# A decoder layer on one core: the FFN's weight chunks begin at eight different places in larger buffers

## The chip, the cores and the metric

The kernel runs on one core of one Trainium2 chip. The metric is the device time of one execution in microseconds (us), as the median of several runs; lower is better. One further execution was taken with the profiler, and all rows below come from it.

## What is computed

One layer with float32 inputs and outputs: 256 tokens, 1024 features. A mixer half (attention and a causal pooling, gated and projected) is added to x, and then the gated FFN that the change touches:

```
h2 = rmsnorm(x, norm_ffn_g)
up = causal_depthwise_conv(h2 @ w_up, conv_w, conv_b)      # w_up: 1024 x 5632
gate, val = jnp.split(up, 2, axis=-1)                      # 2816 each
return x + (jax.nn.silu(gate) * val) @ w_down              # w_down: 2816 x 1024
```

## The kernel before

**Three products for one.** The tensor engine works on `float32r` operands. Each float32 operand is split in two, a high part (rounded to `float32r`) and a low part (the rest), and each product is made of three matmuls: high by high, high by low and low by high (`mm3`, L88; for the down projection L635 to L637). All three add up in one PSUM tile.

**Chunks of weights.** All weights come as chunks of 128 partitions by 2048 float32 (8 KB in a partition), in the fixed sequence `order` (L97 to L107): first q, k and v, then p, g, pool, bp, ba and o of the mixer, then 22 chunks `up` and 11 chunks `dn` of the FFN, mixed. SyncE loads each into one of four `raw` buffers (`load`, L111). ScalarE writes the high part into one of four `whi` buffers (`next_high`, L140, calling `high`, L80), VectorE writes the low part into one of four `wlo` buffers (`next_low`, L151, calling `low`, L84), both in pieces of 1024 columns. `ahead` (L161) stands between the matmul groups and makes the next pieces, so that the split runs ahead of the tensor engine. `chunk` (L169) hands the two buffers of a chunk to the matmuls.

**The FFN loop** (L669). Step i makes two tiles of the up projection, gate and value (`up_tile`, L644): 8 slices of features by 3 matmuls each, so 48 matmuls in a step from one `up` chunk. In each the weights are the stationary operand (128 x 128, brought in by a weight load) and the activations `hhi` and `hlo` the moving one (256 columns). Then it makes the part of the down projection of step i - 3 (`down`, L627): 8 output tiles by 3 matmuls, so 24 matmuls from half of a `dn` chunk; here the weights are stationary too, and the activations `ah` and `al` move. Over the FFN that is 22 x 48 + 22 x 24 = 1584 matmuls. In the q, k and v stage (L278) the roles are the other way round: the activations `xhi` and `xlo` are stationary, and 512 columns of weights move.

**Places in memory.** As the program is built before the change, each `whi` and `wlo` buffer begins 64 bytes past a multiple of 128 bytes (448 past a multiple of 512), and each slice of weights in it lies a multiple of 512 bytes further on. The activations that meet them (`xhi`, `hhi`, `mh`, `poolh`, `ath`, `ah` and their low parts) begin 96 bytes past a multiple of 128 (480 past a multiple of 512). So weights and activations have always the same places against each other within 512 bytes.

Of the kernel before, what the change touches and what calls it, by code (L numbers as in the profile page):

```python
# [9 lines left out]
F32R = mybir.dt.float32r  # L10
# [4 lines left out]
P = 128  # L15
# [17 lines left out]
CH = 2048  # L33
# [19 lines left out]
FFN_AHEAD = 6  # L53
KREADY = 1
FIRST = 2
XCUTS = (1, 2, 4, 6, 8)


@with_exitstack
def hybrid_layer_kernel(ctx: ExitStack, tc: tile.TileContext, xq_d, par_d, wkv_d, wpg_d,  # L60
# [5 lines left out]
    whi_p = ctx.enter_context(tc.tile_pool(name="whi", bufs=WBUFS))  # L66
    wlo_p = ctx.enter_context(tc.tile_pool(name="wlo", bufs=WBUFS))
# [11 lines left out]
    def high(hi, src, scale=1.0):  # L79
        nc.scalar.activation(hi, src, AF.Copy, scale=scale)  # L80
# [16 lines left out]
    order = [("q", None)] * 2 + [("k", wkv_d[c]) for c in range(2)]  # L97
# [10 lines left out]
    raws, his, los = {}, {}, {}  # L108
# [14 lines left out]
    def raw(c, sl):  # L123

        return xq[:, 4 * c + sl.start // 512, S:] if order[c][0] == "q" else raws[c][:, sl]
# [10 lines left out]
    def oldest():  # L136

        return next((c for c in range(len(order)) if c not in spent), len(order))

    def next_high():  # L140
        if at[0] < len(pieces):
            c, sl, first, _ = pieces[at[0]]
            if c - oldest() >= WBUFS:
                return
            at[0] += 1
            if first:
                his[c] = whi_p.tile([P, CH], F32R, tag="whi", name=f"hi_{order[c][0]}{c}")
                los[c] = wlo_p.tile([P, CH], F32R, tag="wlo", name=f"lo_{order[c][0]}{c}")
            high(his[c][:, sl], raw(c, sl))

    def next_low(eager=False):  # L151
# [9 lines left out]
    def ahead(upto=0):  # L161

        next_high()
        next_low()
        if at[1] - sum(p[0] < used[0] for p in pieces) < upto:
            next_high()
            next_low()
# [23 lines left out]
    cut = 0  # L191
    for k in XCUTS:
        end = KD + k * (S + AW)
# [25 lines left out]
    for k in range(KD):  # L219
        if k == 0:  # L220
            nc.vector.tensor_scalar(xhi[:, k, :], xT[:, k, :], gmix[:, k:k + 1], None, op0=ALU.mult)
        else:
            high(xhi[:, k, :], xT[:, k, :], gmix[:, k:k + 1])
        low(xlo[:, k, :], xhi[:, k, :], xT[:, k, :], gmix[:, k:k + 1])
        next_high()
        next_low(eager=True)
# [83 lines left out]
    def to_heads(qg, t, dst, name):  # L310
        pq = bank(f"ps_t{name}{t}")
        flat = qg.rearrange("p h d -> p (h d)")
        for j in range(KA):
            nc.tensor.transpose(pq[:, j * P:(j + 1) * P], flat[:, j * P:(j + 1) * P], ident)
        nc.scalar.activation(dst[:, :, t * P:(t + 1) * P], pq.rearrange("p (j c) -> p j c", c=P), AF.Copy)
# [110 lines left out]
    def scores(hp):  # L426
        ps = ps2.tile([P, 2, 512], F32, tag="ps2", name=f"ps_s{hp}")
        for j in range(2):
            rows = slice(j * DH, (j + 1) * DH)
            nc.tensor.matmul(ps[:, j, P:3 * P], qT[rows, hp, P:S], kT[rows, hp, :], start=True, stop=True)  # L430
            nc.tensor.matmul(ps[:, j, 0:P], qT[rows, hp, 0:P], kT[rows, hp, 0:P], start=True, stop=True)
        sm = tmp.tile([P, 2, 3 * P], F32, tag="big", bufs=4, name=f"sm{hp}")
        nc.vector.tensor_tensor(sm, ps[:, :, 0:3 * P],
                                mask.rearrange("p a b -> p (a b)")[:, None, :].to_broadcast([P, 2, 3 * P]), ALU.add)
        mx = tmp.tile([P, 2, 2], F32, tag="mx", name=f"mx{hp}")
        for t in (1, 0):
            nc.vector.tensor_reduce(mx[:, t, :], sm[:, :, TOK[t]], axis=AX.X, op=ALU.max)
        nc.vector.tensor_scalar(mx, mx, -(DH ** -0.5), None, op0=ALU.mult)
        sums = tmp.tile([P, 2, 2], F32, tag="sums", name=f"sums{hp}")
        for j in range(2):  # L440
            for t in (1, 0):
                nc.scalar.activation(sm[:, j, TOK[t]], sm[:, j, TOK[t]], AF.Exp, bias=mx[:, t, j:j + 1],
                                     scale=DH ** -0.5, accum_out=sums[:, t, j:j + 1])
        rs = tmp.tile([P, 2, 2], F32, tag="rs", name=f"rs{hp}")
        nc.vector.reciprocal(rs, sums)
        for t in (1, 0):
            n = TOK[t].stop - TOK[t].start
            nc.gpsimd.tensor_tensor(sm[:, :, TOK[t]], sm[:, :, TOK[t]],
                                    rs[:, t, :, None].to_broadcast([P, 2, n]), ALU.mult)
        later(4, weigh, hp, sm)  # L450
# [46 lines left out]
    for n in range(2 * KD):  # L497
        if n == KREADY:
            for t in range(NT):
                to_heads(kg[t], t, kT, "k")  # L500
        if n >= FIRST and (n - FIRST) % 4 == 0:
            scores((n - FIRST) // 4)
        if n == 10:
            pool_maps()
            ahead()
        b, c = n // 2, n % 2
# [267 lines left out]
```

## Time and profile before

| | us |
|---|---|
| median of 3 runs | 350.35 (348.51 to 350.55) |
| the profiled execution, its own time | 348.69 |
| its span, first to last instruction | 346.9 |
| its time outside the span | 1.8 |
| TensorE busy (PE) / VectorE (DVE) / ScalarE (ACT) | 340.7 / 261.0 / 195.7 |

In the profile PE is a matmul and PEld a weight load, which runs beside matmuls. The duration shown for a matmul (0.28 us) reaches from its issue to the modelled end of its pipeline, and overlaps those of its neighbours. So the rate of the tensor engine is read from the start of one matmul to the start of the next, and over a long stretch: time from the first start to the last, by the number of matmuls between them.

### The profile page before, as it was taken

The numbers are of one execution on the slowest core, as the hardware profiler recorded it, in microseconds if no ns is written. First come the engines' busy times: TensorE is split into PE (matmuls) and PEld (weight loads), VectorE is DVE, ScalarE is ACT, GpSimd is POOL, SyncE is SP. The second block draws the span as 40 slices with busy tenths as digits, with TensorE's granted clock in tenths as the row PEclk, the third lists the DMA queues.
The fourth block names the chain that finished last, engine by engine and source line by source line (L and its number), as shares of the span: only waits on it lengthen the run. The fifth ranks groups of instructions, "written<-read, shape, count | busy, mean of one in ns | idle before, by whom it ended". The sixth has DMA issues, their size and how long they took to land.

```text
span 346.9 us, 6715 instructions
## 1 busy us (share of the span) xinstructions
PE 340.7 (98%) x2736; PEld 329.2 (95%) x2736; DVE 261.0 (75%) x411; ACT 195.7 (56%) x311; POOL 101.5 (29%) x111
## 2 busy tenths in 40 slices
PE   8999999999999999999999999999999999999996
PEld 6887899999899999999999999999999999999995
DVE  4969889787587585899699877776777777777643
ACT  4956534634748945665367655555555555646420
POOL 1007991112202034586232212121212121212230
PEclk9999999999999999999999999999999999999999
DMA  7985642465272651566257555464636363652003
GB/s 275 419 327 213 222 159 110 150 220 213 69 259 92 242 201 45 175 237 211 109 168 271 188 224 201 164 222 145 242 123 243 131 235 132 232 162 83 0 2 121
DMA packets 10254, 62.76 MB, mean 181 GB/s; under 512 B 1136, under 2 KB 2288, under 8 KB 3312
## 3 DMA queue, kind: packets, MB, share of 16 engines
q1 hardware_dynamic: 10224, 62.34, 49.5%
q8 instruction: 21, 0.34, 0.4%
q14 instruction: 9, 0.07, 0.1%
HBM read 61.29 MB, written 1.05 MB: 180 GB/s over the span
## 4 chain that ended last, share of the span: by engine, by line
PE 80%; DVE 10%; DMA 4%; ACT 2%; issue 2%; SPq 1%; POOL 0%; ACTq 0%
PE ps_up L93 11%; PE ps_up L94 11%; PE ps_up L92 11%; PE ps_d L636 6%; PE ps_d L637 6%; PE ps_d L635 6%; PE ps_g L92 4%; PE ps_g L94 4%; PE ps_g L93 4%; DMA raw_k<-in_wkv 4%; PE ps_v L278 3%; DVE lo_up L84 2%; DVE hlo L86 2%; PE ps_bp L92 1%; PE ps_ba L94 1%
## 5 line engine op out<-in xcount | busy, mean ns | idle before, releaser
L92 PE MATMUL ps_up<-hhi,hi_up 128*128 128x256 f32 x352 | 98.5, 280 | 0.0
L93 PE MATMUL ps_up<-hlo,hi_up 128*128 128x256 f32 x352 | 98.4, 279 | 0.1
L94 PE MATMUL ps_up<-hhi,lo_up 128*128 128x256 f32 x352 | 98.3, 279 | 0.0
L93 PEld LDWEIGHTS ps_up<-hlo,hi_up 128*128 128x128 f32 x352 | 66.2, 188 | 0.4 <-DVE hlo L86 0.4
L92 PEld LDWEIGHTS ps_up<-hhi,hi_up 128*128 128x128 f32 x352 | 66.2, 188 | 0.0
L94 PEld LDWEIGHTS ps_up<-hhi,lo_up 128*128 128x128 f32 x352 | 66.2, 188 | 0.0
L84 DVE TENSOR_TENSOR lo_up<-raw_up,hi_up 128x1024 fp32r<-128x1024 f32 x44 | 55.9, 1273 | 6.1 <-ACT hi_up L80 6.1
L618 POOL TENSOR_TENSOR c_v<-c_g,c_v 128x256 f32<-128x256 f32 x22 | 16.2, 738 | 120.8 <-DVE c_v L601 120.8
L636 PE MATMUL ps_d<-al,hi_dn 128*128 128x256 f32 x176 | 49.1, 279 | 0.0
L635 PE MATMUL ps_d<-ah,hi_dn 128*128 128x256 f32 x176 | 49.1, 279 | 0.0
L637 PE MATMUL ps_d<-ah,lo_dn 128*128 128x256 f32 x176 | 49.1, 279 | 0.0
L80 ACT ACTIVATE hi_up<-raw_up 128x1024 fp32r<-128x1024 f32 x44 | 44.9, 1045 | 0.0
L92 PE MATMUL ps_g<-xhi,hi_g 128*128 128x256 f32 x128 | 36.5, 285 | 0.0
L93 PE MATMUL ps_g<-xlo,hi_g 128*128 128x256 f32 x128 | 35.7, 279 | 0.0
L94 PE MATMUL ps_g<-xhi,lo_g 128*128 128x256 f32 x128 | 35.7, 279 | 0.0
L80 ACT ACTIVATE ah<-c_v 128x256 fp32r<-128x256 f32 x22 | 9.2, 418 | 45.8 <-POOL c_v L618 45.8
L637 PEld LDWEIGHTS ps_d<-ah,lo_dn 128*128 128x128 f32 x176 | 33.1, 188 | 0.0
L635 PEld LDWEIGHTS ps_d<-ah,hi_dn 128*128 128x128 f32 x176 | 33.1, 188 | 0.0
L636 PEld LDWEIGHTS ps_d<-al,hi_dn 128*128 128x128 f32 x176 | 33.1, 188 | 0.0
L606 DVE TENSOR_TENSOR u_v<-ps_up,R 128x256 f32<-128x256 f32 x22 | 9.3, 421 | 26.1 <-PE ps_up L94 26.1
L84 DVE TENSOR_TENSOR lo_dn<-raw_dn,hi_dn 128x1024 fp32r<-128x1024 f32 x22 | 27.8, 1264 | 0.4 <-ACT hi_dn L80 0.4
L642 POOL TENSOR_TENSOR al<-c_v,ah 128x256 fp32r<-128x256 f32 x22 | 23.0, 1045 | 11.6 <-ACT ah L80 11.6
(182 smaller groups left out, 815.8 us busy)
## 6 DMA issues: line engine op xcount, KB each, us to landing
raw_up<-in_wup SPq DMA_DIRECT2D x22, 1024.0 KB, 4.8
raw_dn<-in_wdn SPq DMA_DIRECT2D x11, 1024.0 KB, 4.8
raw_g<-in_wpg SPq DMA_DIRECT2D x8, 1024.0 KB, 4.8
raw_o<-in_wout SPq DMA_DIRECT2D x4, 1024.0 KB, 4.8
xq<-in_xq SPq DMA_DIRECT2D x3, 768.0 KB, 7.4
raw_v<-in_wkv SPq DMA_DIRECT2D x2, 1024.0 KB, 14.1
raw_p<-in_wpg SPq DMA_DIRECT2D x2, 1024.0 KB, 6.3
raw_bp<-in_wbp SPq DMA_DIRECT2D x2, 1024.0 KB, 4.8
```

The lines of the kernel that those rows point to most:

```text
L80: nc.scalar.activation(hi, src, AF.Copy, scale=scale)
L84: nc.vector.tensor_tensor(lo, src, hi.bitcast(F32), ALU.subtract)
L92: nc.tensor.matmul(out, sh, mh, start=start, stop=False, **kw)
L93: nc.tensor.matmul(out, sh, ml, start=False, stop=False, **kw)
L94: nc.tensor.matmul(out, sl, mh, start=False, stop=stop, **kw)
L278: nc.tensor.matmul(pt[t], sx[:, k, t * P:(t + 1) * P], wx[:, sl], start=k == 0 and sx is xhi and wx is hi, stop=k == KD - 1 and wx is lo)
L606: nc.vector.tensor_tensor(u, ps[:, 0:S], R2, ALU.mult)
L618: nc.gpsimd.tensor_tensor(uc[1], g[1], uc[1], ALU.mult)
L635: nc.tensor.matmul(o, hi[:, sl], acch[i], start=first, stop=False, skip_group_check=True)
L636: nc.tensor.matmul(o, hi[:, sl], accl[i], start=False, stop=False, skip_group_check=True)
L637: nc.tensor.matmul(o, lo[:, sl], acch[i], start=False, stop=i == KF - 1, skip_group_check=True)
L642: nc.gpsimd.tensor_tensor(accl[i], act_i, acch[i].bitcast(F32), ALU.subtract)
```

## The change

The tiles of `whi` and `wlo` become 32 columns (128 bytes) wider for all chunks, and each chunk takes a window of 2048 columns in its tile. For `up` and `dn` the window begins at one of eight offsets in turn, the first chunk of its kind at 0 bytes, the second at 32, then 16, 48, 8, 96, 64, 80 and again from 0; `up` and `dn` count apart. For all other chunks it begins at 0. The high and the low part of a chunk have the same offset.

```diff
 FIRST = 2
+
+SHIFT = (0, 32, 16, 48, 8, 96, 64, 80)
 XCUTS = (1, 2, 4, 6, 8)
...
             if first:
-                his[c] = whi_p.tile([P, CH], F32R, tag="whi", name=f"hi_{order[c][0]}{c}")
-                los[c] = wlo_p.tile([P, CH], F32R, tag="wlo", name=f"lo_{order[c][0]}{c}")
+                name = order[c][0]
+                turn = sum(order[i][0] == name for i in range(c))
+                off = SHIFT[turn % len(SHIFT)] // 4 if name in ("up", "dn") else 0
+                his[c] = whi_p.tile([P, CH + 32], F32R, tag="whi", name=f"hi_{name}{c}")[:, off:off + CH]
+                los[c] = wlo_p.tile([P, CH + 32], F32R, tag="wlo", name=f"lo_{name}{c}")[:, off:off + CH]
             high(his[c][:, sl], raw(c, sl))
```

As the programs are built, every engine runs the same instructions in the same order with the same waits, before and after; only addresses differ. The buffers now lie 8320 bytes apart instead of 8192, so each still begins 64 bytes past a multiple of 128. All activations move up by 1024 bytes and keep their place within any 1024. The `raw` buffers stay where they were.

How the 33 chunks of the FFN fall on the offsets (48 matmuls each):

| offset, bytes | weights begin, past a multiple of 128 | `up` chunks | `dn` chunks |
|---|---|---|---|
| 0 | 64 | 3 | 2 |
| 32 | 96 | 3 | 2 |
| 16 | 80 | 3 | 2 |
| 48 | 112 | 3 | 1 |
| 8 | 72 | 3 | 1 |
| 96 | 32 | 3 | 1 |
| 64 | 0 | 2 | 1 |
| 80 | 16 | 2 | 1 |

## Rows read from the trace of the kernel before

**Rows 1.** The page: busy time of each engine, its share of the span and its instructions, the busy share of TensorE and the granted TensorE clock in 40 slices of the span.

```profile
span 346.9 us, 6715 instructions
PE 340.7 (98%) x2736; PEld 329.2 (95%) x2736; DVE 261.0 (75%) x411; ACT 195.7 (56%) x311; POOL 101.5 (29%) x111
...
PE   8999999999999999999999999999999999999996
...
PEclk9999999999999999999999999999999999999999
```

**Rows 2.** The windows of the FFN: its entry, the first steps, the steady steps, the last down projections and the end. Columns: window, its length, busy time and instructions of each engine, granted clock, DMA share, GB/s.

```profile
core 0: us, PE busy (x) PEld busy (x) DVE busy (x) ACT busy (x) POOL busy (x), PEclk, DMA share, GB/s
156.60:166.20 9.60, 9.03 (x75) 8.60 (x74) 8.35 (x12) 4.82 (x6) 6.13 (x6) 1.00 0.62 215
166.20:181.05 14.85, 14.85 (x128) 14.82 (x127) 12.71 (x24) 8.00 (x14) 3.83 (x5) 1.00 0.33 111
181.05:332.25 151.20, 151.20 (x1298) 151.20 (x1297) 112.54 (x164) 87.72 (x129) 33.92 (x38) 1.00 0.49 174
332.25:343.60 11.35, 11.35 (x98) 11.17 (x96) 5.15 (x12) 1.44 (x3) 1.47 (x2) 1.00 0.18 59
```

**Rows 3.** The timeline of the matmuls at the first and at the last start of the steady stretch, in order of time. Columns: start, duration, engine, line, operation, tile and operands, shapes.

```profile
180.95 0.28 PE L94 MATMUL ps_up<-hhi,lo_up 128*128 128x256 f32 x1
181.06 0.28 PE L635 MATMUL ps_d<-ah,hi_dn 128*128 128x256 f32 x1
181.19 0.28 PE L636 MATMUL ps_d<-al,hi_dn 128*128 128x256 f32 x1
...
332.15 0.28 PE L94 MATMUL ps_up<-hhi,lo_up 128*128 128x256 f32 x1
332.26 0.28 PE L635 MATMUL ps_d<-ah,hi_dn 128*128 128x256 f32 x1
```

**Rows 4.** The timeline of the matmuls of the first k chunk, where the weights move in 512 columns; each row is two matmuls, and there are 12 such rows from the first to the last.

```profile
17.24 0.63 PE L278 MATMUL ps_k<-hi_k,xhi 128*128 128x512 f32 x2
17.70 0.63 PE L278 MATMUL ps_k<-hi_k,xlo 128*128 128x512 f32 x2
...
22.37 0.63 PE L278 MATMUL ps_k<-lo_k,xhi 128*128 128x512 f32 x2
22.84 0.50 PE L238 MATMUL ps_n<-ones,vn 128*128 128x1 f32 x4
```

**Rows 5.** The timeline of the weight loads around the token sums of the FFN's norm (`ps_n`), whose matmuls move a single column, so that the weight loads follow one another with almost nothing between them.

```profile
162.46 0.19 PEld L94 LDWEIGHTS ps_up<-hhi,lo_up 128*128 128x128 f32 x1
162.57 0.53 PEld L238 LDWEIGHTS ps_n<-ones,ss 128*128 128x128 f32 x4
163.02 0.19 PEld L92 LDWEIGHTS ps_up<-hhi,hi_up 128*128 128x128 f32 x1
```

**Rows 6.** Groups of weight loads by line and form. Columns: busy time, mean ns of one, idle time before. In the first three the stationary operand is weights, in the others activations (`xhi`, `ss`).

```profile
L92 PEld LDWEIGHTS ps_up<-hhi,hi_up 128*128 128x128 f32 x352 | 66.2, 188 | 0.0
L94 PEld LDWEIGHTS ps_up<-hhi,lo_up 128*128 128x128 f32 x352 | 66.2, 188 | 0.0
L635 PEld LDWEIGHTS ps_d<-ah,hi_dn 128*128 128x128 f32 x176 | 33.1, 188 | 0.0
...
L278 PEld LDWEIGHTS ps_k<-lo_k,xhi 128*128 128x128 f32 x16 | 3.0, 188 | 0.7
...
L238 PEld LDWEIGHTS ps_n<-ones,ss 128*128 128x128 f32 x4 | 0.5, 190 | 0.0
```

**Rows 7.** Groups of VectorE by line and form in the steady stretch, 181.05 to 332.25 us: the low parts, and the taps of the convolution, which read and write `c` from 4 (L600) or 8 bytes (L601) past where its tile begins.

```profile
L84 DVE TENSOR_TENSOR lo_up<-raw_up,hi_up 128x1024 fp32r<-128x1024 f32 x36 | 44.8, 1248 | 6.1 <-ACT hi_up L80 6.1
L84 DVE TENSOR_TENSOR lo_dn<-raw_dn,hi_dn 128x1024 fp32r<-128x1024 f32 x20 | 24.9, 1243 | 0.4 <-ACT hi_dn L80 0.4
...
L601 DVE SCALAR_TENSOR_TENSOR c_v<-u_v,par,c_v 128x254 f32<-128x254 f32 x18 | 8.7, 482 | 0.6
L600 DVE SCALAR_TENSOR_TENSOR c_v<-u_v,par,c_v 128x255 f32<-128x255 f32 x18 | 8.6, 478 | 0.0
```

**Rows 8.** The same view of the first 20 us: the same operation where all operands begin where their tiles do.

```profile
L86 DVE SCALAR_TENSOR_TENSOR xlo<-xq,xhi 128x256 fp32r<-128x256 f32 x8 | 3.8, 481 | 1.1 <-ACT xhi L80 1.1
```

**Rows 9.** Groups of ScalarE in the steady stretch: the high parts.

```profile
L80 ACT ACTIVATE hi_up<-raw_up 128x1024 fp32r<-128x1024 f32 x35 | 35.7, 1044 | 0.0
L80 ACT ACTIVATE hi_dn<-raw_dn 128x1024 fp32r<-128x1024 f32 x20 | 20.0, 1045 | 0.0
```

**Rows 10.** The chain of work that ended last, in order of time, at the FFN's entry. Columns: start, share of the chain in us, what.

```profile
149.95 1.13 DVE lo_up L84
...
152.17 0.61 DVE lo_up L84
...
154.60 1.35 DVE lo_up L84
...
159.47 1.35 DVE lo_up L84
160.82 0.22 DVE hlo L86
161.04 0.46 issue
161.50 2.90 DVE lo_up L84 x2
...
166.52 0.12 PE ps_up L92
```

## The prediction

> **What bounds the kernel now.** First the page [rows 1]: the tensor engine is busy for 340.7 of 346.9 us, the matmul row shows 8 and 9 tenths in all slices but the last, and the granted clock is 9 in every slice, that is the level of 2.4 GHz all the way. VectorE has 75% and ScalarE 56%. So the question for a change of addresses is first of all what it does to the rate of the matmuls, and only then what it does to the engines that write the buffers.
>
> Then the windows of the FFN, where the change is [rows 2]. In the steady steps, from 181.05 to 332.25 us, the tensor engine is busy for 151.20 of 151.20 us: no wait for weights, for activations or for PSUM. Here alone the time is purely the number of matmuls by the spacing of their starts. The timeline gives that spacing [rows 3]: the first matmul of the stretch starts at 181.06, and the one that opens the last down projections at 332.26. Between them lie 18 steps of 48 + 24 matmuls, 1296 in all; 151.20 us / 1296 = 116.67 ns. A matmul moves 256 columns, which at 2.4 GHz are 106.67 ns. So each matmul of the FFN costs 10.0 ns more than its columns, and this is the one thing that a better placed operand could win. Over the FFN's 1584 matmuls it is 15.8 us.
>
> Whose cost are the 10 ns? If they came from the weight load (one in each matmul) meeting the moving stream, they would be a sum for each weight load. The k stage tells this apart [rows 4]: there a matmul moves 512 columns for one weight load. 12 rows of two lie between 17.24 and 22.84 us: 5.60 us / 24 = 233.3 ns, against 213.3 ns for 512 columns. That is 20.0 ns more, twice the 10.0 ns, with the same single weight load, and it is exactly twice 116.67. So the loss goes with the columns that move, 35 cycles for 32 columns, and not with the loads. In this stage the weights (64 bytes past a multiple of 128) move and the activations (96 past) stand; in the FFN it is the other way round. The rate of a column is the same. So the loss does not ask, either, at which of these two places the moving operand begins.
>
> How near is the weight load to being the bound itself? The timeline of the norm's sums shows it nearly bare [rows 5]: its matmuls move one column, and from the first of its four loads at 162.57 to the load after them at 163.02 there are 0.45 us, 112.5 ns for a load, what little the single columns take included. So a load of 128 columns takes at most 112.5 ns of its port, and the matmuls' 116.67 ns cover it with a margin of 4.2 ns. This is small, and it is the number to watch. The shown durations do not differ by place: 188 ns for weights at 64 past, 188 for `xhi` at 96 past, 190 for the sums' `ss` at 96 past [rows 6].
>
> **The change part by part.** It adds no instruction and moves none, adds no wait and no byte of transfer: the `raw` buffers, their loads and the number of buffers stay. Five things can have a price.
>
> *The moving stream of the FFN.* The activations keep their places within 1024 bytes, so a stream whose cost goes with its own columns costs the same 116.67 ns: 0 us. From below, nothing can be taken off here unless the loss is a matter of both operands, which is the faster rival.
>
> *The weight loads.* At the offsets 0, 32, 64 and 96 the slices begin at 64, 96, 0 and 32 past a multiple of 128, all multiples of 32. A place 96 past is in the trace: the `ss` loads that gave the 112.5 ns lie there. So these 17 chunks (11 `up`, 6 `dn`) stay under 116.67: 0 us. At 16, 48, 80 and 8 (16 chunks, 11 `up` and 5 `dn`, 768 matmuls) no row shows a load. From below 0, since a load that is hidden cannot win anything. From above, a slice is 512 bytes, and a start out of line touches one more piece of memory: 17 pieces of 32 bytes for 16 make 112.5 x 17/16 = 119.5 ns, 2.9 over the stream, 768 x 2.9 = 2.2 us; 9 pieces of 64 for 8 make 126.6, 9.9 over, 7.6 us. Pieces of 64 fit badly, as `ss` at 96 past is already across them at 112.5. I take 0, since the nearest rows (188 against 190 ns for different places, and the same rate of the moving stream at two places) know no price for a place; 2.2 us is kept for the range.
>
> The Trainium skill, "SBUF — State Buffer", section "Specifications (TRN2)", speaks against the change: it gives SBUF lines of 16 bytes, and each access that crosses to a new line pays. By that page the starts at 8 bytes past a line (4 chunks) would touch 33 lines for 32, which with the row's 112.5 ns is an estimate of 116.0 ns, still under the stream's 116.67 and so nothing; all other offsets are whole lines. No row of this kernel shows a load out of line.
>
> *The low parts on VectorE.* They read and write the shifted buffers: 56 pieces and 69.7 us of the steady stretch [rows 7], in which VectorE has 112.5 of 151.2 us [rows 2]. It would take 38.7 us more, 55% on every piece, to make VectorE the bound. The convolution's taps, which begin 4 or 8 bytes past their tile, give the price: 478 ns for 255 and 482 ns for 254 elements [rows 7], against 481 for 256 in place [rows 8]. A few ns on 1245: 0 us in the steady steps. In the entry the chain runs over `lo_up` [rows 10], where there is no slack, but some seven pieces at a few ns make under 0.1 us.
>
> *The high parts on ScalarE*: 1044 ns each [rows 9], with 87.7 of 151.2 us busy. Even 10% on 55 pieces is 6 us of 63 us idle: 0 us.
>
> *The wider pitch.* All the mixer's chunks still begin 64 past a multiple of 128, only no longer at the same place in 512. The 35 for 32 held with the moving operand at 64 past and at 96 past, so another multiple of 128 should cost as little: 0 us.
>
> **The sum** is 0 us: a span of 346.9 us as now. The profiled execution took 348.69 us, 1.66 under the median of 350.35, and the runs lie from 348.51 to 350.55; a repeat of the same program thus scatters by some 2 us. I set the forecast at the median, 350.35 us.
>
> **The rivals.** *Faster: the loss is a meeting of the two operands.* All rows of before have weights and activations 32 bytes apart within 512. If the 10 ns came of that, any other distance might end it, and 28 of the 33 chunks get another distance. The weight load then is the bound at 112.5 ns: 4.2 ns x 28 x 48 = 5.6 us, 344.7 us. Over 1% (3.5 us) needs 18 of the 28 chunks. Against it stands the k stage: twice the loss with one load [rows 4]. For it, that the k stage has the same distance, so that the distance was never tried. The Trainium skill, "SBUF — State Buffer", section "Who interferes with whom", speaks against this rival as well: it gives TensorE two independent read ports, one for the moving operand and one for weight loads. The trace agrees as far as the loss goes with columns at 20.0 to 10.0 ns. Chance 0.11.
>
> *Slower: the weight load becomes the bound at the odd places.* The place is every matmul of the 16 chunks at 16, 48, 80 and 8 bytes; the margin is 4.2 ns. At 126.6 ns for a load it is 7.6 us, 358.0 us. It decides from 116.67 + 3500/768 = 121.2 ns on, that is from a load that is 8% slower. If only the 8-byte chunks (192 matmuls) suffer, it takes 18 ns over the stream for the same 1%. For it: the margin is small and no row has such a start. Against it: no place that the trace has shows a price. Chance 0.13.
>
> *The change does not do what it says* is no case here: `chunk` hands out the shifted windows themselves, so the high part, the low part and all matmuls of a chunk use them.
>
> **How the numbers follow.** Under 1% (3.5 us) a measurement of this kernel, whose runs scatter by 2 us, can hardly tell from no change. Forecast, no change: 0.76, own range 348.5 (the lowest run) to 352.6 (350.35 + 2.2). Slower 0.13, faster 0.11. The range runs from 347.0, where about half of the moved chunks have reached the load's rate (350.35 - 2.8, and the scatter), to 354.0, just past where the slower rival decides; it leaves out the full prices on both sides, together under 0.2.
>
> **What would show it.** In the profile after, the steady stretch should again hold 1296 matmuls in 151.2 us, and each chunk by itself should show 116.67 ns from start to start, whatever its offset. That is the finest test: eight offsets in one trace. If the slower rival holds, only the chunks at 16, 48, 80 and 8 (or 8 alone) show spacings above 116.67, and the starts of the weight loads, not the matmuls, set them. If the faster one holds, the chunks off offset 0 show less than 116.67, and the chunks at 0 in the same loop do not. The low parts should stay at 1245 ns and the high parts at 1044. What would make the prediction wrong is a spacing that differs by chunk; a change of the time with 116.67 everywhere would have to come from the entry (156.6 to 166.2 us) or from the scatter of the runs.

## The result, and the profile after

| | before | after |
|---|---|---|
| median, us | 350.24 (348.44 to 350.59, 9 runs) | 351.8 (9 runs, 8 of them from 351.55 to 351.84) |
| ratio after / before | | 1.0056, 95% interval 1.0037 to 1.0075 |
| profiled execution, its own time | 348.69 | 351.81 |
| its span | 346.9 | 350.0 |

The change makes the kernel 0.6% slower. Disturbed executions are left out of the comparisons: of the changed kernel one (417.96 us at a granted clock of 0.756), and of four kernels below, whose clock was full, those in the slower of two levels, which are told where they stand.

Before itself has two levels, some at 348.4 to 348.8 us and some at 350.1 to 350.6; 6 of these 9 runs lie at the upper. After has one. Against the lower level, in which the profiled execution of before lies, the change costs 3.2 us.

The page of after, busy time and granted clock (answers to [rows 1]):

```profile
span 350.0 us, 6715 instructions
...
PE 343.9 (98%) x2736; PEld 332.1 (95%) x2736; DVE 261.0 (75%) x411; ACT 195.8 (56%) x311; POOL 102.3 (29%) x111
...
PEclk9999999999999999999999999999999999999999
```

The same 2736 matmuls, at the same clock, take 3.2 us more of the tensor engine's busy time; VectorE and ScalarE are as they were to 0.1 us. The windows of the FFN, cut at the same matmuls as in [rows 2]:

```profile
core 0: us, PE busy (x) PEld busy (x) DVE busy (x) ACT busy (x) POOL busy (x), PEclk, DMA share, GB/s
156.60:166.20 9.60, 9.18 (x76) 8.77 (x75) 8.75 (x12) 4.82 (x6) 6.45 (x7) 1.00 0.64 217
166.20:181.77 15.57, 15.54 (x128) 15.49 (x129) 13.03 (x24) 8.03 (x15) 4.10 (x5) 1.00 0.35 118
181.77:335.09 153.32, 153.32 (x1298) 153.32 (x1297) 112.18 (x164) 87.73 (x129) 34.39 (x37) 1.00 0.48 172
335.09:346.50 11.41, 11.41 (x98) 11.40 (x96) 5.15 (x12) 1.44 (x3) 1.46 (x2) 1.00 0.17 57
```

In the steady stretch the tensor engine is again busy all the time: no wait has come in. The timeline of its matmuls (answers to [rows 3]), columns as there: the first matmuls of three `out` chunks of the mixer, which the change moves only by the pitch; the first of the steady stretch; of three `up` chunks the first matmul and the first one behind the chunk; and the last start of the stretch.

```profile
134.57 0.28 PE L94 MATMUL ps_out<-mh,hi_o 128*128 128x256 f32 x1
...
140.27 0.28 PE L94 MATMUL ps_out<-mh,hi_o 128*128 128x256 f32 x1
...
145.88 0.28 PE L94 MATMUL ps_out<-mh,hi_o 128*128 128x256 f32 x1
...
181.78 0.28 PE L640 MATMUL ps_d<-ah,hi_dn 128*128 128x256 f32 x1
...
193.11 0.28 PE L94 MATMUL ps_up<-hhi,hi_up 128*128 128x256 f32 x1
...
198.55 0.28 PE L640 MATMUL ps_d<-ah,hi_dn 128*128 128x256 f32 x1
...
227.04 0.28 PE L94 MATMUL ps_up<-hhi,hi_up 128*128 128x256 f32 x1
...
232.80 0.28 PE L640 MATMUL ps_d<-ah,hi_dn 128*128 128x256 f32 x1
...
261.38 0.28 PE L94 MATMUL ps_up<-hhi,hi_up 128*128 128x256 f32 x1
...
267.04 0.28 PE L640 MATMUL ps_d<-ah,hi_dn 128*128 128x256 f32 x1
...
335.10 0.28 PE L640 MATMUL ps_d<-ah,hi_dn 128*128 128x256 f32 x1
```

From 181.78 to 335.10 are 153.32 us, by 1296 matmuls 118.3 ns, against 116.67 before. So 2.12 us are lost in the stretch, 0.72 ahead of it (181.78 against 181.06) and 0.26 behind it (350.0 - 335.10 = 14.90 against 346.9 - 332.26 = 14.64): 3.1 us, the whole difference of the spans.

And the spacing differs by chunk. The chunk at 193.11 (offset 96) takes 5.44 us / 48 = 113.3 ns, less than any spacing of before; the one at 227.04 (offset 32) 5.76 / 48 = 120.0; the one at 261.38 (offset 96 again) 5.66 / 48 = 117.9. The two unshifted `out` chunks take 5.70 / 48 = 118.8 and 5.61 / 48 = 116.9: their buffers begin 64 and 192 past a multiple of 256. All `up` chunks from the third step on, in ns, from starts to the single ns (the rows above are rounded to 10 ns):

| offset, bytes | first turn | second | third |
|---|---|---|---|
| 0 | | 117.9 (0) | 116.8 (0) |
| 32 | | 120.0 (32) | 118.5 (160) |
| 16 | 119.9 (144) | 119.9 (16) | 119.9 (16) |
| 48 | 118.3 (48) | 120.0 (176) | 120.0 (176) |
| 8 | 117.7 (8) | 117.8 (8) | 118.4 (8) |
| 96 | 113.3 (224) | 117.8 (224) | 113.7 (96) |
| 64 | 118.2 (64) | 118.4 (64) | |
| 80 | 118.1 (208) | 117.8 (80) | |

In brackets stands the place of the chunk within 256 bytes as the program is built, counted from that of before. The buffers lie 8320 bytes apart, so every second one is 128 bytes further within 256, and the eight offsets become the thirteen places of this table. Two offsets with two spacings are simply two places each (32 and 160, 48 and 176); the 113.3 and 117.8 at 224 are two spacings of one place.

The low parts in the stretch (VectorE groups by line and form, answers to [rows 7]), 1244 ns against 1248 and 1243, rule VectorE out:

```profile
L86 DVE TENSOR_TENSOR lo_up<-raw_up,hi_up 128x1024 fp32r<-128x1024 f32 x36 | 44.7, 1244 | 6.1 <-ACT hi_up L82 6.1
L86 DVE TENSOR_TENSOR lo_dn<-raw_dn,hi_dn 128x1024 fp32r<-128x1024 f32 x20 | 24.9, 1244 | 0.4 <-ACT hi_dn L82 0.4
```

### The profile page after: what moved, and what is told of

The parts are those of the page before. It is cut to its first block, busy times and chain, and to the rows that moved or that the text cites. A ratio compares the mean times of both kernels' runs of the same rounds, so it can differ in the third digit from the quotient of the medians.

```text
span 350.0 us, 6715 instructions
## 1 busy us (share of the span) xinstructions
PE 343.9 (98%) x2736; PEld 332.1 (95%) x2736; DVE 261.0 (75%) x411; ACT 195.8 (56%) x311; POOL 102.3 (29%) x111
## 4 chain that ended last, share of the span: by engine, by line
PE 80%; DVE 10%; DMA 3%; ACT 2%; issue 2%; SPq 1%; POOL 0%; ACTq 0%
PE ps_up L95 11%; PE ps_up L94 11%; PE ps_up L96 11%; PE ps_d L640 6%; PE ps_d L642 6%; PE ps_d L641 6%; PE ps_g L94 4%; PE ps_g L95 4%; PE ps_g L96 4%; DMA raw_k<-in_wkv 3%; PE ps_v L283 3%; DVE lo_up L86 2%; DVE hlo L88 2%; PE ps_bp L94 1%; PE ps_ba L96 1%
## 5 line engine op out<-in xcount | busy, mean ns | idle before, releaser
L647 POOL TENSOR_TENSOR al<-c_v,ah 128x256 fp32r<-128x256 f32 x22 | 23.8, 1080 | 11.6 <-ACT ah L82 11.6
```

What stands on the lines that cost most here:

```text
L647: nc.gpsimd.tensor_tensor(accl[i], act_i, acch[i].bitcast(F32), ALU.subtract)
```

## The experiments

The theory (P) is that the spacing is set by the place of the weights against the moving activations, and that one place can hold more than one spacing. The rivals: a price only for starts that are out of line with some piece of memory; a price for changing the place from chunk to chunk; contention from the engines that write the buffers (E); and chance, a spacing that asks for no place. "Offset" below is counted from where the weights begin in before; unless said, the activations keep their place within 256 bytes. A run of before stands beside each group: 348.77 (19 runs), then 348.73 (9), 348.69 (8) and 349.04 (11) us.

**The kernel before again**, no edit.

> The kernel before, unchanged, for a second trace of it. Theory P (place): a matmul's spacing follows from where its weights begin against its moving activations within some power of two of bytes, 256 as the trace after suggests; here all chunks have one place, so every chunk should show 116.67 ns again, as in the first trace. Theory S (state): the spacing wanders from execution to execution whatever the places; then this trace shows chunks at 117 to 120 ns as the changed kernel did.

348.82 us in one run, 116.67 ns in each chunk behind the FFN's entry. Of the 19 runs of before beside it, 7 lie at 350.26 to 350.48 us and 12 at 348.60 to 348.91.

**The pitch alone**, without an offset.

```diff
-his[c] = whi_p.tile([P, CH], F32R, ...)
+his[c] = whi_p.tile([P, CH + 32], F32R, ...)[:, 0:CH]        # lo the same
```

> Tiles 32 columns wider as in the change, all windows at 0: the buffers lie 8320 bytes apart, so two of the four begin 192 and two 64 bytes past a multiple of 256 (activations: 224). Theory P: chunks in the buffers at 192 stay at 116.67 ns, chunks in those at 64 take 117.4 to 118.8 ns, as the mixer's unshifted chunks do after the change; over some 1584 FFN and 800 mixer matmuls, half of them, that is 1 to 2 us more: 351 to 352.5 us. Rival Q (only the starts out of line by 8 or 16 bytes cost, by way of the weight load): no chunk changes, 350.2 us.

349.92 us (349.82 to 350.08, 10 runs), ratio 1.0019 (1.0 to 1.0037). That is over a microsecond less than expected: 6 of the 18 `up` chunks in the steady stretch, and not half of them, lie in a buffer at 64, and they take 117.3 or 118.7 ns. Two neighbouring `up` chunks, first matmul and the first one behind each:

```profile
235.05 0.28 PE L92 MATMUL ps_up<-hhi,hi_up 128*128 128x256 f32 x1
...
240.65 0.28 PE L635 MATMUL ps_d<-ah,hi_dn 128*128 128x256 f32 x1
...
243.50 0.28 PE L92 MATMUL ps_up<-hhi,hi_up 128*128 128x256 f32 x1
...
249.20 0.28 PE L635 MATMUL ps_d<-ah,hi_dn 128*128 128x256 f32 x1
```

5.60 / 48 = 116.7 ns in a buffer at 192 past a multiple of 256, 5.70 / 48 = 118.8 in one at 64. Both are 64 past a multiple of 128, so that is not the measure; and starts that are all multiples of 64 bytes differ, so no penalty on odd starts is needed.

**A pitch that keeps the place within 256 bytes**: as above with `CH + 64`.

> Tiles 64 columns wider, all windows at 0: the buffers lie 8448 bytes apart, a multiple of 256, and the activations move up by 2048 bytes. Theory P: all chunks keep their place within 256 bytes and stay at 116.67 ns; the time is that of the kernel before, 348.4 to 350.6 us. Rival R (larger buffers, a wider pitch or moved activations cost by themselves): at least as slow as the change, 351.8 us.

350.22 us (348.55 to 350.49, 10 runs), ratio 1.0009 (0.9986 to 1.0032): the two levels of before, with one run between them (349.48). Its profiled execution (350.26 us) lies in the upper one, the first and last matmul of the steady stretch:

```profile
181.07 0.28 PE L635 MATMUL ps_d<-ah,hi_dn 128*128 128x256 f32 x1
...
333.71 0.28 PE L635 MATMUL ps_d<-ah,hi_dn 128*128 128x256 f32 x1
```

152.64 us / 1296 = 117.8 ns, where before had 116.67 at the same place within 256 bytes. So the upper level of this kernel is a second spacing of one place: 1.1 ns more in the FFN's 1584 matmuls is 1.7 us, the distance of the levels. A trace of before's own layer in it comes with the groups of several sizes below.

**The place by itself**: behind the FFN, with no other engine at work, groups of 48 matmuls (their products unused) on one chunk, at 32 offsets, 8 bytes apart, in two orders.

```diff
+    for turn in (1, 13):
+        for g in range(32):
+            off = 2 * (g * turn % 32)
...
+            for k in range(48):
+                nc.tensor.matmul(pr[:, 0:S], hw[:, k % 8 * 128 + off:k % 8 * 128 + off + P], hhi[:, k % 8, :], start=True, stop=True)
```

> The kernel before with 64 groups of 48 matmuls added behind the FFN, at a time when no other engine works: the moving operand is hhi (224 past a multiple of 256), the stationary one a window of the last chunk's high part that begins 0, 8, ... 248 bytes further, once in ascending order and once in steps of 104 bytes. Their products are used by nothing. Theory P: the spacing differs from group to group between 113 and 120 ns with no other engine at work, and mostly agrees between the two orders. Rival Q: 116.67 ns at all multiples of 32 and more at the others. Rival E (other engines' traffic in the buffers makes the difference): 116.67 ns or less in all groups.

`off` counts elements of 4 bytes. The timeline of some groups in the first order (each row one group, the letter ahead of the `b` its offset: a is 0, b 8, e 32, f 40, m 96, n 104):

```profile
343.19 5.77 PE L709 MATMUL probe_ab<-hhi,hi_dn 128*128 128x256 f32 x48
348.79 5.81 PE L709 MATMUL probe_bb<-hhi,hi_dn 128*128 128x256 f32 x48
...
365.71 5.91 PE L709 MATMUL probe_eb<-hhi,hi_dn 128*128 128x256 f32 x48
371.46 5.71 PE L709 MATMUL probe_fb<-hhi,hi_dn 128*128 128x256 f32 x48
...
411.23 5.62 PE L709 MATMUL probe_mb<-hhi,hi_dn 128*128 128x256 f32 x48
416.69 5.85 PE L709 MATMUL probe_nb<-hhi,hi_dn 128*128 128x256 f32 x48
```

From one group's start to the next: 5.60 us at 0, 5.75 at 32, 5.46 at 96, which is 116.7, 119.8 and 113.8 ns with what lies between two groups; inside a group 116.67, 120.0 and 113.3. Over all places 113.3 (96, 120 and 200 in both orders) to 120 (32, 136, 144, 192, 248), once 121.6 (56, in the other order 118.6) and once 123.3 (8, in the other order 117.8). At 224 the two orders gave 117.8 and 113.3, as the change did. The whole range of the FFN's spacings is here with VectorE and ScalarE at 0.00 us of work and a DMA share of 0.00 (from 347.5 us to the end), so the rival E falls; and among the places with 120 are multiples of 64 and 32 (192, 32) as well as of 8 alone (136, 248).

**One offset for the whole FFN**, the best and the worst of the change's own, at the pitch that keeps the place.

```diff
+off = 24 if order[c][0] in ("up", "dn") else 0
+his[c] = whi_p.tile([P, CH + 64], F32R, ...)[:, off:off + CH]     # lo the same
```

24 elements are 96 bytes; the other kernel has 8 for 32 bytes.

> Tiles 64 columns wider (the buffers keep one place within 256 bytes) and all up and dn chunks at one offset, 96 bytes; the mixer's chunks at 0. The probe showed 113.33 ns at this offset in both orders. Theory P (the place of the weights against the moving activations, within 256 bytes, sets which repeating pattern of spacings the matmuls fall into): the FFN runs at 113.33 ns throughout, 3.3 ns less on 1584 matmuls, 5.3 us less: 343.5 us if the kernel before is in its 116.67 pattern at 348.6 us, 1.8 us more gain against its 117.83 pattern. Rival Q (weight loads at odd starts): no gain can come from a start, 348.5 us or more. Rival T (it is the changing from place to place that costs, not the place): 116.67 as before, 348.6 to 350.5 us.

343.81 us (343.71 to 343.95, 4 runs), ratio 0.9861 (0.9846 to 0.9875). The first and last matmul of the stretch:

```profile
180.74 0.28 PE L636 MATMUL ps_d<-ah,hi_dn 128*128 128x256 f32 x1
...
327.78 0.28 PE L636 MATMUL ps_d<-ah,hi_dn 128*128 128x256 f32 x1
```

147.04 us / 1296 = 113.5 ns. It is faster than both kernels.

> As the run with 96 bytes, but all up and dn chunks at 32 bytes, where the weights begin at the same place within 128 bytes as the activations. The probe showed 120.0 ns in both orders. Theory P: 120.0 ns throughout the FFN, 3.3 ns more on 1584 matmuls, 5.3 us more than the 116.67 pattern: 353.9 us. Rival T: 116.67 ns, 348.6 to 350.5 us. Rival Q: the start is a multiple of 32, so no change.

353.72 us (353.56 to 353.74, 4 runs), ratio 1.0144 (1.0128 to 1.0159), the same rows:

```profile
181.46 0.28 PE L636 MATMUL ps_d<-ah,hi_dn 128*128 128x256 f32 x1
...
336.98 0.28 PE L636 MATMUL ps_d<-ah,hi_dn 128*128 128x256 f32 x1
```

155.52 us / 1296 = 120.0 ns. A start at a multiple of 32 bytes that never changes costs more than the change with its eight offsets: neither a price for odd starts nor one for changing places says that. Two kernels that differ in 64 bytes of place are 9.9 us apart.

**The activations moved instead**, weights as in before, so that the difference is that of offset 96.

```diff
+gap = ctx.enter_context(tc.tile_pool(name="gap", bufs=1)).tile([P, 40], F32, name="gap")
```

The gap is 160 bytes and lies ahead of the activations.

> Weights and their buffers as in the kernel before; a gap of 160 bytes ahead of the activations moves all of these, so that weights begin 64 bytes past the activations within 256, the same difference as with weights moved by 96. If only the difference counts: 113.33 ns in the FFN and in the mixer (g, p, bp, ba, o), 3.3 ns less on some 2400 matmuls, 8 us less: 340.5 us. If the place of the weights by itself counts: 116.67 ns, 348.6 us. If that of each operand by itself counts, some other spacing.

343.05, 343.15 and 343.36 us, and 349.83 and 349.89; ratio from the first three 0.9844 (0.9825 to 0.9864). The profiled execution is one of the latter:

```profile
180.72 0.28 PE L636 MATMUL ps_d<-ah,hi_dn 128*128 128x256 f32 x1
...
333.36 0.28 PE L636 MATMUL ps_d<-ah,hi_dn 128*128 128x256 f32 x1
```

152.64 us / 1296 = 117.8 ns, at a clock of 0.998. The same execution had 113.3 ns in the mixer. The first of the 96 matmuls of `ba`, and the first one behind them:

```profile
122.80 0.28 PE L93 MATMUL ps_ba<-ath,hi_ba 128*128 128x256 f32 x1
...
133.68 0.28 PE L93 MATMUL ps_out<-mh,hi_o 128*128 128x256 f32 x1
```

10.88 us / 96 = 113.3 ns. So the gain comes by moving either operand: the difference counts, not the place of the weights. And this difference has two spacings, 113.3 and 117.8. In this execution the one gave way to the other at the FFN's entry, where waits and the sums of the norm break the stream. The better times are some 2.7 us over the 340.5 that were expected, which counted the mixer's matmuls at full gain: even with 113.3 ns in the mixer the FFN began only 1.0 us earlier than in before (155.69 against 156.66).

**Size and repetition**, groups as above: load widths of 128, 64 and 32 columns, 256, 512 and 128 moving columns, both operands moved together, and one place again and again behind 1 to 10 short matmuls.

```diff
+            w = k % 8 * 128 + off // 4
+            m = k % (1536 // n) * n + mo // 4
+            nc.tensor.matmul(pr[0:cols, 0:n], hw[:, w:w + cols], wide[:, m:m + n], start=True, stop=True)
```

> The kernel before with groups of matmuls added behind the FFN, whose products nothing uses. Offsets of the weights 0, 32 and 96 bytes; weight loads of 128, 64 and 32 columns for 256 that move; 512 that move; 128 that move; both operands moved together by 32, 64 and 128 bytes; and repeats of one place with another number of short matmuls ahead of each. Theory C (the reads of the weight load and of the moving operand collide, and the place decides how often): with loads of 64 and 32 columns the spacing falls towards 106.7 to 109 ns and no longer depends on the offset; with both operands moved together the spacing stays that of the difference; repeats at one place show a few fixed values (116.67 and 117.83 at offset 0). Theory M (the moving stream loses 3 cycles in 32 columns by itself, as the prediction had it): 116.67 ns for shorter loads too. At 512 columns the prediction's 233.3 ns should come back at offset 0; theory C has the same loss for one load whatever moves, so about 223 ns, unless a load spreads over the longer stream.

Some of the groups (a is offset 0, b 32; `full` is 128 columns loaded and 256 moved, `half` and `quarter` load 64 and 32, `long` and `short` move 512 and 128; `again_c` is offset 96):

```profile
363.11 5.76 PE L711 MATMUL probe_long_a<-hhi,hi_dn 128*128 128x512 f32 x24
368.70 5.47 PE L711 MATMUL probe_short_a<-hhi,hi_dn 128*128 128x128 f32 x48
374.01 5.96 PE L711 MATMUL probe_full_b<-hhi,hi_dn 128*128 128x256 f32 x48
379.80 5.61 PE L711 MATMUL probe_half_b<-hhi,hi_dn 128*64 128x256 f32 x48
385.25 5.61 PE L711 MATMUL probe_quarter_b<-hhi,hi_dn 128*32 128x256 f32 x48
390.69 5.63 PE L711 MATMUL probe_long_b<-hhi,hi_dn 128*128 128x512 f32 x24
396.16 5.47 PE L711 MATMUL probe_short_b<-hhi,hi_dn 128*128 128x128 f32 x48
...
522.75 3.04 PE L711 MATMUL probe_again_c<-hhi,hi_dn 128*128 128x256 f32 x24
525.91 2.95 PE L711 MATMUL probe_again_c<-hhi,hi_dn 128*128 128x256 f32 x24
```

At offset 32 the full group takes 5.79 us to the next start, `half` and `quarter` 5.45 and 5.44: inside the groups 120.0 against 113.3 and 113.3 ns. The moving columns are the same, so the weight load takes part in the loss. How is not so simple: at offset 0 the three widths gave 117.8, 119.0 and 117.3 ns, at 96 all three 113.3, so the spacing still goes with the offset and does not fall to 106.7 to 109 ns, as theory C had it. 512 columns take about 227 ns at offset 32 and 233 at 0 and 96. 128 columns take 5.31 us / 48 = 110.6 ns at offset 0, near the bare load of [rows 5]. With both operands moved together by 32, 64 and 128 bytes, difference 0 gave 116.67 or 117.8, difference 32 gave 120 and difference 96 gave 117.8 each time (unmoved 113.3, its other spacing): again the difference. Repeated ten times, offset 0 gave 116.67 eight times and 117.8 twice, offset 96 gave 113.3 eight times and 117.8 twice, offset 224 gave 117.8 ten times: the two rows of `again_c`, 3.04 and 2.95 us for the same 24 matmuls, are 0.09 / 23 = 4 ns apart for each spacing. So one place has few spacings, and a stream takes up one of them where it begins.

The layer ahead of these groups is that of before, to the address. Its FFN, the first and the last start of the steady stretch:

```profile
182.16 0.28 PE L635 MATMUL ps_d<-ah,hi_dn 128*128 128x256 f32 x1
...
334.80 0.28 PE L635 MATMUL ps_d<-ah,hi_dn 128*128 128x256 f32 x1
```

152.64 us / 1296 = 117.8 ns, behind a mixer at 116.67: the second spacing of before, in a trace of its own. The matmuls ahead of the FFN are the same in all executions of before, so they alone do not pick the spacing.

**The change's offsets at the pitch that keeps the place**: the change with `CH + 64` for `CH + 32`.

> The change with tiles 64 instead of 32 columns wider: the eight offsets as they were, but all buffers at one place within 256 bytes. Theory P: the mixer back at 116.67 ns; in the FFN each chunk at a spacing that the probe showed for its offset (113.3 at 96, 116.7 at 0, 117.3 to 118.3 at 16, 8, 48, 64 and 80, 120 at 32; by the number of chunks at each, 117.5 on average), 1.3 us over the 116.67 pattern: about 349.9 us, and two chunks of one offset may show two spacings. If the offsets alone make the whole loss of the change: 351.8 us.

350.98 us (350.78 to 351.27, 5 runs), ratio 1.0061 (1.0041 to 1.008): 1.1 us over what was expected: in the profiled execution (351.27 us) the chunks at 16 bytes ran at 119.6 to 119.9 ns where the groups had 117.3, and at 96 bytes one of three `up` chunks and the `dn` chunk at 117.7 to 117.9 for 113.3. Over the lower level of 348.6 us the pitch alone costs 1.3 us, the offsets alone 2.4, both 3.2: they don't add, because the pitch changes the places at which the offsets fall.

**One offset for all chunks**, the mixer's too: `off = 24`, `30` or `50` (96, 120 and 200 bytes, the three places with 113.3 in both orders).

> Tiles 64 columns wider and all chunks, the mixer's too, at 96 bytes. Theory P with two patterns at this place (113.33 and 117.79 ns): where the 113.33 pattern holds in the FFN and in most of the mixer, 341 to 343.5 us; in executions in which the FFN falls into the other one, about 349.9 us as in the run with moved activations. If weights moved forward and activations moved by the rest of 256 are the same thing, the times and patterns of that run come back.

343.45, 343.56 and 343.57 us, and 350.15; ratio from the first three 0.9846 (0.9817 to 0.9874). The profiled execution is the last, with 117.8 ns throughout the FFN: the two levels of the kernel with moved activations.

> As the run with all chunks at 96 bytes, but at 120, where the probe showed 113.33 ns in both orders. Theory P: 113.33 ns in FFN and mixer, 341 to 343 us. Rival Q (starts that are no multiple of 32 slow the weight load): slower than 348.6 us.

342.94, 343.05, 347.47 and 348.31 us, ratio without the last 0.9873 (0.9801 to 0.9945). Two of the four are some 5 us over the 341 to 343 that were expected. The profiled execution, 348.31 us, has 116.7 ns in the FFN and the mixer, where the groups had 113.3 at this place.

> As the run with all chunks at 96 bytes, but at 200, where the probe also showed 113.33 ns in both orders. Theory P: 113.33 ns in FFN and mixer, 341 to 343 us; if the place has a single pattern, all executions within 0.3 us of each other. Rival Q: slower than 348.6 us.

355.48 us (354.37 to 355.66, 4 runs), ratio 1.018 (1.0146 to 1.0215): a miss, by 12 us. The stretch:

```profile
183.11 0.28 PE L636 MATMUL ps_d<-ah,hi_dn 128*128 128x256 f32 x1
...
338.63 0.28 PE L636 MATMUL ps_d<-ah,hi_dn 128*128 128x256 f32 x1
```

155.52 us / 1296 = 120.0 ns, where the groups alone had 113.3 at the same place. A place does not have one spacing, and a short stream of one sequence does not tell which one the kernel gets.

**The entry**: the FFN's own sequence (weights by activations: high by high, high by low, low by high), 24 matmuls at 8 offsets, entered behind 1, 2, 3, 5 and 7 short matmuls, with 128, 64 and 32 columns loaded.

```diff
+            w, mv = ((hw, hhi), (hw, hlo), (lw, hhi))[k % 3]
+            at = k // 3 * 256 + off // 4
+            nc.tensor.matmul(pr[0:cols, 0:S], w[:, at:at + cols], mv[:, k // 3, :], start=True, stop=True)
```

> The kernel before with groups behind the FFN of 24 matmuls in the FFN's own sequence (high by high, high weights by low activations, low by high), at each of the change's eight offsets, each entered five times behind 1, 2, 3, 5 or 7 short matmuls, and all of it for weight loads of 128, 64 and 32 columns. Nothing uses the products. If place and entry together pick the pattern: each offset shows the same one to three spacings whatever the entry, among them 116.67 and 117.8 at 0, 120 at 32, 113.3 and 117.8 at 96. If the weight load takes part in it: other spacings at the same offset for loads of 64 and 32 columns, and 120 gone at 32. If the moving stream alone makes the spacing: no difference between the three widths.

Offset 96 with full loads, twelve matmuls apart in the group behind 1 short matmul and in that behind 3:

```profile
457.64 0.28 PE L713 MATMUL probe_full_h<-hhi,hi_dn 128*128 128x256 f32 x1
...
459.05 0.28 PE L713 MATMUL probe_full_h<-hhi,hi_dn 128*128 128x256 f32 x1
...
463.82 0.28 PE L713 MATMUL probe_full_h<-hhi,hi_dn 128*128 128x256 f32 x1
...
465.18 0.28 PE L713 MATMUL probe_full_h<-hhi,hi_dn 128*128 128x256 f32 x1
```

1.41 us / 12 = 117.5 ns and 1.36 / 12 = 113.3: same instructions, same place, other entry. Counted over twelve matmuls in the middle of each group, full loads gave 119.5 to 120.0 at offset 32 at all five entries, 116.7 at 0, and at 96 113.3 three times and 117.8 twice. Over the 40 groups of a width the mean is 117.7 ns with 128 columns loaded, 116.6 with 64 and 115.0 with 32; but at offset 96 half loads gave 118.9 to 119.1 and at offset 0 117.8 to 119.0, more than full ones, so it is not the length of the load alone. No group is under 113.3.

**Mixer at 120, FFN at 96 bytes.** `off = 24 if order[c][0] in ("up", "dn") else 30`.

> Tiles 64 columns wider, up and dn chunks at 96 bytes, all others at 120. The FFN at 113.33 ns and the mixer between 113.33 and 116.67: 341 to 343.8 us. If the pattern of the FFN hangs on how it is entered, and the other pattern of the mixer brings the FFN into 117.79 ns, executions at some 348 to 350 us appear, which the run with the mixer at 0 did not have.

343.19, 343.21, 343.56 and 343.65 us, and 349.13 and 349.23; ratio from the first four 0.9824 (0.9792 to 0.9855). At its best it is no more than 0.6 us faster than the FFN alone at 96 bytes, and a third of its runs fall to the other level. In its four runs the kernel with the FFN alone at 96 bytes never did, which is too few to say that it cannot.

## Why the prediction was wrong, point by point

1. **What bounds the kernel** was right: after is again busy in all of the steady stretch, and the time is the number of matmuls by their spacing. The finest test named there, the spacing of each chunk, gave the answer.
2. **"So the loss goes with the columns that move, 35 cycles for 32 columns, and not with the loads. [...] So the loss does not ask, either, at which of these two places the moving operand begins."** This is the step that failed. The doubling from 116.67 to 233.3 ns [rows 3, 4] holds at offset 0; at 32 bytes 256 columns take 120.0 ns and 512 take 227, at 96 they take 113.3 and 233. One place, at which the two numbers agreed, was read as a law. In its place the runs show a spacing that goes with the difference of the two operands' places: 343.81 us with all weights of the FFN at 96 bytes, 353.72 with all at 32. And weights and activations that change roles at the same two places keep their difference up to its sign, so the k stage had nothing to say on it. The rows held a warning: the starts at 181.06, 181.19 and 181.30 [rows 3] are 0.13 and 0.11 apart, where an even price per column would make even steps. To the single ns the steps of before repeat in fours, about 113, 116, 118 and 120 ns, 116.67 on average.
3. **The terms that came from it**, "0 us" for the moving stream, for the 17 chunks at multiples of 32 and for the wider pitch, were wrong. Against the lower level the pitch alone cost 1.3 us, the offsets alone 2.4, both 3.2. The 2.2 us kept for the 16 chunks at 16, 48, 80 and 8 was of the right size for the wrong reason: the chunks at 32 cost as much as those at 16. That 351.8 us lies within the prediction's own range, 348.5 to 352.6, is luck too: spacings from 113.3 to 120.0 ns happen to average 118.3 in the steady stretch, near the 116.67 of before.
4. **The weight load "hidden" under 116.67 ns** was half right. Loads with little between them follow each other in 110.6 to 112.5 ns, but at offset 32 narrower loads bring the matmuls from 120.0 to 113.3 ns: a load that is shorter than the stream still takes part in its rate. By the Trainium skill, "SBUF — State Buffer", section "Who interferes with whom", TensorE's two read ports are independent. By that rule alone a narrower load would not have changed the loss; here it did, by 6.7 ns, and the measurement decides.
5. **VectorE and ScalarE at 0 us** was right: 1244 ns for a low part, and 195.8 us against 195.7 for ScalarE.
6. **The faster rival**, a meeting of the two operands, had the mechanism right. Its rate of 112.5 ns is near the 113.3 that a good place gives, and its 344.7 us near the 343.8 of one offset of 96 bytes. What it had wrong is that any other difference would end the meeting: most of the change's differences are worse than that of before (117.7 to 120.0 ns), and the one good offset had 113.3 and 113.7 in two of its three turns, 117.8 in the other. Nor is the load the bound behind it: loads of 32 columns did not bring the spacing under 113.3 either.
7. **The slower rival**, loads that take more pieces from odd starts, had the sign right and the mechanism wrong: 8 bytes gave 117.7 to 118.4 ns, 32 bytes 118.5 to 120.0, and in the groups 120 and 200 bytes, which are 8 past a multiple of 16, gave 113.3.
8. **The scatter of "some 2 us"** was taken for noise. It is two spacings of one place, 116.67 and 117.8 ns, and with more runs it shows: of the 56 runs of before 54 lie from 348.4 to 348.9 us or from 350.1 to 350.6.

What is shown is that the difference of the two places narrows the spacing to few values, that a stream takes up one of them where it begins, and that the weight load takes part. Which one it takes up is not explained: another number of short matmuls ahead changed it, and so did another execution of the same kernel. What in the memory or in the tensor engine makes the repeating patterns, why no spacing under 113.3 ns (272 cycles for 256 columns) was seen, and how an entry could be forced is not settled either.

## What to carry to other kernels

Where the tensor engine is busy all the time, compare the spacing of matmuls chunk by chunk, and try a few places of the stationary operand against the moving one within 256 bytes: here 113.3 to 120.0 ns, 343.8 to 353.7 us. Keep one good difference for a whole stream rather than many, measure it in the kernel itself and several times, since a place can hold two spacings. And a law that is read from rows of one place only says nothing of another.

## What the runs showed of the hardware

- Matmuls of 256 `float32r` columns with a load of 128 columns each take 113.3 to 120.0 ns (once 121.6 and once 123.3) at the full clock, by the difference of the operands' places within 256 bytes.
- The spacing is not single-valued: 116.67 or 117.8 at the difference of before, 113.3 or 117.8 at offset 96, 113.3 (groups) or 120.0 (kernel) at offset 200. What decides between them is open; where the place stayed, the spacing of the steady stretch held to its end, and it changed at the FFN's entry (116.67 to 117.8 in one execution, 113.3 to 117.8 in another).
- The width of the weight load changes the spacing though the load fits under the stream: means of 117.7, 116.6 and 115.0 ns for 128, 64 and 32 loaded columns. At offset 0 it went the other way, 117.8 to 119.0 ns with 64 columns against 116.7 with 128.
